# Index scores behind each query tile, a wider top-k search and six places for split weights in a hybrid decoder layer

## The chip, the cores and the metric

The kernel runs on one core of one Trainium2 chip, in one launch. The metric is the device time in microseconds; the kernel before took 826.19 us (median of three runs, 826.02 to 827.07).

## What is computed

One layer of an autoregressive trunk: 512 tokens of width 1024, float32, with a fixed memory of 256 tokens. The mixer has three head groups that read the same projection; this is its core, with the part that the change touches written out:

```python
h = layer_norm(x)
gq, gk, gv, glr, gg, dq, dk, dv, iq, ik, iw, sq, sk, sv = split(h @ w_in)
# indexer, per block of 128 query tokens
rel = relu(einsum('bthd,bsd->bths', iq, ik))          # 8 indexer heads of 64
isc = einsum('bths,bth->bts', rel, iw) * idx_scale
isc = where(causal, isc, -inf)
_, idx = top_k(isc, 128)                              # min(256, 512 // 4)
# sparse attention on the selected keys, less slope * distance
o_dsa = softmax(q @ k_sel - slopes * dist) @ v_sel @ w_uv
o_gla = gated_linear_attention(gq, gk, gv, glr, gg)   # 4 heads, chunks of 64
o_sb  = stick_breaking(sq, sk, sv)                    # 5 heads, strictly causal
h = layer_norm(ALPHA * h + concat(o_gla, o_dsa, o_sb) @ w_out)
h = layer_norm(ALPHA * h + mem_attention(h, mem))
h = layer_norm(ALPHA * h + relu(h @ w_up + b_up) ** 2 @ w_down + b_down)
```

Block 0 of the indexer needs no search: it has 128 keys, and all causal ones are taken.

## The kernel before

**Precision.** Weights and activations are split in a high and a low part. A product of two such operands is three matmuls on TensorE (PE): high x high, high x low, low x high (`mm3`). A weight chunk is loaded as a raw tile (`r_...`), copied to its high part (`h_...`, by ScalarE (ACT), GpSimd (POOL) or VectorE (DVE)), and the low part (`l_...`) is raw minus high (DVE or POOL). Raw tiles live in pool `wr` (4 places), high and low parts in `wh` and `wl` (5 places each, L383 and L384), temporaries of 512 floats in `half` (8 places), pages of 1024 floats in `pages` (31), and PSUM banks in `psum` (8). `page`, `temp` and `bank` take a tile from these.

**Order.** The code doesn't issue instructions as it runs. Every call on an engine is recorded by `Program` with the clock value of its place in the text; `nc.clock` can be set back or ahead, so that a piece of work is spread between others. `issue` then plans all instructions: it goes through time, picks for each engine the recorded operation that can start first by a table of prices and lags, at most 560 clock units ahead of the oldest that is not yet placed, holds a tile back until its pool has a place, and for operations recorded with `either` picks the engine. The instructions are emitted in that order from a single line, L356, which therefore stands in every row of the trace; each engine runs its queue in order and waits on semaphores. DMAs are issued from SyncE (SP).

**Stages.** The input layer norm, with its transposes, fills the first 25 us. Then come, by the order in the text: the indexer key and weights (`ik`, `iw`), the indexer queries (`iq`, four tiles of two heads each), the GLA values and gate rank (`gv_glr`), the GLA query-key tiles (`gqk_tile`, three of them), the score pages, the gates, GLA, stick-breaking (`sq`, `sk`, `ps_z`, `sp`), sparse attention (`ps_s`, `ps_pt`), output projection, memory attention (`ps_ms`, `ps_mpt`) and the MLP (`ps_up`, `ps_dn`).

**The indexer.** For each of the blocks j = 1, 2, 3 the page `acc` of that block, 128(j+1) columns wide, gathers eight heads: a pair of matmuls into a bank `ps_idx`, a relu on ACT into `r`, a multiply-add on DVE. All eight heads of all blocks are recorded behind the first query-key tile. `top_k` then finds 128 of the entries in 16 pairs of steps on DVE (MAX gives eight maxima, MATCH_REPLACE strikes them out), 17 clock steps a block, spaced by `TOPK_STRETCH` = 10 units; the mask that results copies key distances (`rel`) into the page `E`, which the sparse attention reads.

**GLA keys.** `gqk_tile` copies its bank to `gqk` and sends rows of it by DMA into `gqT` and `gkT`. `keT` is an exponential of the gate times `gkT`; `ps_ke` is its transpose on PE. `r_gg` and `r_sv` are weights of the gates and of the stick-breaking values, loaded on the same SP queue.

The lines of the changed parts:

Of the kernel before, what the change touches and what calls it, by code (L numbers as in the profile page):

```python
# [364 lines left out]
def trunk_kernel(ctx: ExitStack, tc: tile.TileContext, x, mem, ln_in_g, ln_in_b, w_in, gate_w2,  # L365
# [35 lines left out]
    def bank(name, shape=(512,)):  # L401
        return psum.tile([128] + list(shape), F32, name)
# [8 lines left out]
    def mm(o, a, b, start, stop):  # L411
        nc.tensor.matmul(o, a, b, start=start, stop=stop, skip_group_check=True)
# [27 lines left out]
                            base=0, channel_multiplier=1)  # L440


    scan_mask = cst.tile([128, 512], F32, "scan_mask")
    nc.gpsimd.memset(scan_mask, 1.0)
    nc.gpsimd.memset(scan_mask[:, 0:512:64], 0.0)
    ps = bank("ps_warm")
# [19 lines left out]
    def split_weights(raw, hi, lo):  # L466
        split(hi, lo, raw, slack[0])
# [95 lines left out]
    for t in range(NT):  # L563
        ln_hat(x_pg[t], "in")
        if t % 2:
            ln_transposed(x_pg, *gb_cols["in"], hT, t - 1, 2)


    rel = cst.tile([128, 512], F32, "rel")
    nc.gpsimd.iota(rel, pattern=[[1, 512]], base=-384, channel_multiplier=-1, allow_small_or_imprecise_dtypes=True)  # L570
    cmask_f = cst.tile([128, 128], F32, "cmask_f")
    nc.gpsimd.memset(cmask_f, 1.0)
    nc.gpsimd.affine_select(out=cmask_f, in_=cmask_f, pattern=[[1, 128]], compare_op=OP.is_ge, fill=0.0,
                            base=0, channel_multiplier=-1)
    nc.gpsimd.memset(cmask_f[0:64, 64:128], 0.0)
    cmask = cst.tile([128, 128], U32, "cmask")
    nc.vector.tensor_copy(cmask, cmask_f)
    tri_f = cst.tile([128, 128], F32, "tri_f")
    nc.gpsimd.memset(tri_f, -1.0)
    nc.gpsimd.affine_select(out=tri_f, in_=tri_f, pattern=[[-1, 128]], compare_op=OP.is_ge, fill=0.0,  # L580
                            base=0, channel_multiplier=1)
    negtri = cst.tile([128, 128], F32R, "negtri")
    nc.vector.tensor_copy(negtri, tri_f)
    ones_f = cst.tile([128, 128], F32, "ones_f")
    nc.gpsimd.memset(ones_f, -1.0)
    negones = cst.tile([128, 128], F32R, "negones")
    nc.vector.tensor_copy(negones, ones_f)
# [82 lines left out]
    gqT = page([2, T], F32, "gqT")  # L670
    gkT = page([2, T], F32, "gkT")
    for t in (gqT, gkT):
        nc.gpsimd.memset(t, 0.0)
    def gqk_tile(i):
        ps = proj_T([(C_GQ + 128 * i, 128, 0)], "gqk")
        raw = temp("gqk")
        for r0, r1 in (((0, 64), (64, 128)) if i == 1 else ((0, 128),)):
            is_q = 128 * i + r0 < C_GK
            nc.scalar.activation(raw[r0:r1], ps[r0:r1], AF.Copy, scale=GLA_DK ** -0.5 if is_q else 1.0)

        for n in range(2 * GLA_H):
# [9 lines left out]
    E_pg = [page([1024], F32, "E012"), page([512], F32, "E3")]
    E = [E_pg[0][:, 0:128], E_pg[0][:, 128:384], E_pg[0][:, 384:768], E_pg[1][:, 0:512]]
    accs = {}
    for j in range(1, NT):
        n = 128 * (j + 1)
        acc = temp(f"acc{j}")
        accs[j] = acc
        for h in range(IDX_H):
            ps = bank("ps_idx")
            for i in range(2):  # L700
                mm(ps[:, :n], iq[h][:, 128 * j:128 * j + 128], ik[:, i, 0:n], i == 0, i == 1)
            r = temp("r")
            nc.scalar.activation(r[:, :n], ps[:, :n], AF.Relu)
            if h == 0:
                nc.vector.tensor_scalar(acc[:, :n], r[:, :n], iw[:, j, 0:1], None, op0=OP.mult)
            else:
                nc.vector.scalar_tensor_tensor(acc[:, :n], r[:, :n], iw[:, j, h:h + 1], acc[:, :n],
                                               op0=OP.mult, op1=OP.add)
        nc.gpsimd.affine_select(out=acc[:, n - 128:n], in_=acc[:, n - 128:n], pattern=[[-1, 128]],
                                compare_op=OP.is_ge, fill=MASKED, base=0, channel_multiplier=1)  # L710

    def top_k(j):

        n = 128 * (j + 1)
        acc = accs[j]
        for _ in range(TOPK // 8):
            m8 = tiny(8, "m8")
            nc.vector.max(m8, acc[:, :n])
            nc.vector.match_replace(out=acc[:, :n], in_to_replace=m8, in_values=acc[:, :n], imm_value=TAKEN)
            yield  # L720
        msk = temp("msk", dtype=U32)
        nc.vector.tensor_scalar(msk[:, :n], acc[:, :n], -2e38, None, op0=OP.is_lt)
        nc.gpsimd.memset(E[j], MASKED)
        nc.vector.copy_predicated(E[j], msk[:, :n], rel[:, 384 - 128 * j:512])
        yield
# [22 lines left out]
    for p in range(2):  # L748
# [502 lines left out]
    def first_weights(i):  # L1251
        r0, r1 = raw_down(i, 0), raw_down(i, 1)
        t3 = temp("t3")
        any_tt(t3, r1[:, R], r0[:, R], OP.subtract)
        any_tt(r0[:, R], r0[:, R], r0[:, L], OP.subtract)
        kept = dram.tile([128, 1024], F32, f"t13_{i}")
        nc.sync.dma_start(kept[:, L], r0[:, R])
        nc.sync.dma_start(kept[:, R], t3)
        sums.append(kept)
        any_tt(r1[:, R], r1[:, R], r0[:, R], OP.subtract)  # L1260
        any_tt(r1[:, L], r1[:, R], r1[:, L], OP.subtract)
        hi = [wh_pool.tile([128, n], F32R, f"h_dn{n}") for n in (512, 1024)]
        lo = [wl_pool.tile([128, n], F32R, f"l_dn{n}") for n in (512, 1024)]
        split_weights(r0[:, L], hi[0], lo[0])
        split_weights(r1, hi[1], lo[1])
        return [(hi[0], lo[0]), (hi[1][:, R], lo[1][:, R]), (hi[1][:, L], lo[1][:, L])]
# [150 lines left out]
```

## Time and profile before

| | |
|---|---|
| median of three runs | 826.19 us (826.02 to 827.07) |
| profiled execution, device time | 825.4 us |
| its span in the trace | 823.6 us |
| granted TensorE clock, mean | 0.991 of full speed |
| PE busy | 792.5 us, 96% |
| DVE busy | 631.3 us, 77% |
| ACT busy | 329.2 us, 40% |
| POOL busy | 158.2 us, 19% |

The span is from the first to the last instruction of the profiled execution; the device time is 1.8 us longer. Busy PE is not PE at its peak: a stall of a matmul in its pipeline counts as busy. The waits of an engine tell what its idle time ended with. A clock of 1.00 is the full 2.4 GHz.

### The profile page before, as it was taken

To read this page: it belongs to the slowest core of one execution; us is meant where nothing else is said; L and a number is where in the kernel's file an instruction comes from. 1 tells how busy PE (TensorE), PEld (TensorE's weight loads), DVE (VectorE), ACT (ScalarE), POOL (GpSimd) and SP (SyncE) were. 2 spreads that over 40 slices of the span, in tenths; PEclk is the share of its full clock that TensorE was granted. 3 is DMA by queue.
4 is the path that set the end of the run, shared out by engine and by line. 5 is a ranking of instruction groups with operands and counts; after the bars stand their busy time and mean duration, and the time that the engine had idled before them with its cause. 6 is when DMAs were issued, how large, how long until landed. Compare 5 with 4: busy or idle time off the path is not lost.

```text
span 823.6 us, 11289 instructions
## 1 busy us (share of the span) xinstructions
PE 792.5 (96%) x4177; PEld 662.8 (80%) x4177; DVE 631.3 (77%) x1111; ACT 329.2 (40%) x634; POOL 158.2 (19%) x173
## 2 busy tenths in 40 slices
PE   7999999999999899989999989999999999899995
PEld 5997769777877888888878889888888888678884
DVE  7737999997649983886553799767777776798778
ACT  4506634577535540233330143333323232585420
POOL 5320142354622210227340210000000000110001
PEclk9999999999999999999999999999999999999998
DMA  8520331603244534023322024645546555467532
GB/s 239 137 53 15 100 94 27 179 9 103 75 152 159 165 120 150 27 77 103 114 92 77 26 77 142 217 154 186 197 137 214 196 174 175 138 219 240 196 126 103
DMA packets 99927, 106.70 MB, mean 130 GB/s; under 512 B 10448, under 2 KB 79136, under 8 KB 99872
## 3 DMA queue, kind: packets, MB, share of 16 engines
q1 hardware_dynamic: 97344, 99.00, 38.1%
q10 hardware_dynamic: 2528, 6.98, 2.5%
q8 instruction: 33, 0.54, 0.3%
q14 instruction: 22, 0.18, 0.1%
HBM read 94.69 MB, written 10.49 MB: 128 GB/s over the span
## 4 chain that ended last, share of the span: by engine, by line
PE 68%; DVE 16%; issue 2%; ACT 1%; DMA 1%; POOL 0%; DVEq 0%; ACTq 0%; POOLq 0%
PE ps_up L356 20%; PE ps_dn L356 17%; PE ps_wmo L356 4%; PE ps_wo L356 4%; PE ps_q L356 3%; DVE res L356 2%; PE ps_km L356 2%; PE ps_z L356 2%; DVE acc L356 2%; PE ps_vm L356 2%; PE ps_gg L356 1%; PE ps_dq L356 1%; PE ps_mo L356 1%; DVE m L356 1%; DVE s L356 1%
## 5 line engine op out<-in xcount | busy, mean ns | idle before, releaser
L356 PE MATMUL ps_up<-h2T,h_up 128*128 128x512 f32 (+1 forms) x576 | 161.1, 366 | 0.0
L356 PEld LDWEIGHTS ps_up<-h2T,h_up 128*128 128x128 f32 x576 | 104.0, 189 | 17.6 <-DVE h2T L356 0.2
L356 PE MATMUL ps_up<-h2T,l_up 128*128 128x512 f32 (+1 forms) x288 | 104.8, 366 | 0.5 <-DVE l_up L356 0.5
L356 ACT ACTIVATE ur<-ps_up,gb_all 128x512 f32<-128x512 f32 x32 | 22.1, 690 | 108.7 <-PE ps_up L356 108.7
L356 PEld LDWEIGHTS ps_up<-h2T,l_up 128*128 128x128 f32 x288 | 54.1, 189 | 9.5 <-DVE l_up L356 0.7
L356 PE MATMUL ps_dn<-h_dn,a 128*128 128x512 f32 x192 | 59.3, 389 | 0.0
L356 DVE TENSOR_TENSOR l_dn<-r_dn,h_dn 128x1024 fp32r<-128x1024 f32 (+1 forms) x44 | 45.2, 1026 | 5.1 <-ACT h_dn L356 3.7
L356 PE MATMUL ps_dn<-h_dn,ends 128*128 128x512 f32 x128 | 47.7, 396 | 0.7 <-DVE ends L356 0.7
L356 POOL TENSOR_TENSOR a<-keep,a 128x1024 fp32r<-128x1024 f32 x1 | 4.1, 4067 | 228.3 <-PE ps_dn L356 228.3
L356 PE MATMUL ps_q<-h1T,h_wmq 128*128 128x256 f32 (+1 forms) x192 | 45.7, 329 | 0.0
L356 ACT ACTIVATE h<-ps_lt,gb_all 128x256 f32<-128x256 f32 x20 | 10.2, 566 | 85.6 <-PE ps_lt L356 84.8
L356 PEld LDWEIGHTS ps_dn<-h_dn,a 128*128 128x128 f32 x192 | 36.0, 188 | 7.5
L356 PE MATMUL ps_wmo<-h_wmo,oT 128*128 128x512 f32 x128 | 40.7, 393 | 0.0
L356 DVE TENSOR_TENSOR l_up<-r_up,h_up 128x1024 fp32r<-128x1024 f32 x32 | 38.9, 1220 | 2.2 <-ACT h_up L356 0.5
L356 PE MATMUL ps_wo<-h_wo,mix 128*128 128x512 f32 x128 | 40.3, 392 | 0.0
L356 PE MATMUL ps_dn<-l_dn,a 128*128 128x512 f32 x96 | 37.3, 389 | 0.0
L356 PEld LDWEIGHTS ps_q<-h1T,h_wmq 128*128 128x128 f32 x192 | 32.9, 197 | 2.5 <-DVE h1T L356 0.2
L356 PE MATMUL ps_q<-h1T,l_wmq 128*128 128x256 f32 (+1 forms) x96 | 31.3, 330 | 0.5 <-DVE ve_mix L356 0.5
L356 DVE TENSOR_SCALAR h_up<-r_up 128x1024 fp32r<-128x1024 f32 x17 | 11.8, 692 | 26.1 <-PE ps_up L356 22.6
L356 PEld LDWEIGHTS ps_dn<-h_dn,ends 128*128 128x128 f32 x128 | 24.5, 192 | 6.3 <-DVE ends L356 1.2
L356 PEld LDWEIGHTS ps_wo<-h_wo,mix 128*128 128x128 f32 x128 | 24.0, 188 | 4.9
L356 PEld LDWEIGHTS ps_wmo<-h_wmo,oT 128*128 128x128 f32 x128 | 24.0, 188 | 4.8
(408 smaller groups left out, 2095.6 us busy)
## 6 DMA issues: line engine op xcount, KB each, us to landing
r_dn<-in_w_down_dram SPq DMA_DIRECT2D x48, 512.0 KB, 4.3
r_up<-in_w_up_dram SPq DMA_DIRECT2D x32, 512.0 KB, 4.5
r_t<-t SPq DMA_DIRECT2D x16, 512.0 KB, 3.6
r_kvv<-in_w_mem_kv_dram SPq DMA_DIRECT2D x8, 512.0 KB, 4.0
r_kvk<-in_w_mem_kv_dram SPq DMA_DIRECT2D x8, 512.0 KB, 3.6
r_wo<-in_w_out_dram SPq DMA_DIRECT2D x8, 512.0 KB, 4.4
r_wmq<-in_w_mem_q_dram SPq DMA_DIRECT2D x8, 512.0 KB, 5.0
r_wmo<-in_w_mem_o_dram SPq DMA_DIRECT2D x8, 512.0 KB, 3.4
```

What stands on the lines that cost most here:

```text
L356: f(*[real(a) for a in args], **{k: real(a) for k, a in kwargs.items()})
```

## The change

- `wh` and `wl` have six places each instead of five.
- Five constants give up their own room: `scan_mask` and `rel` share one page (`masks`), and `cmask_f`, `cmask`, `tri_f`, `ones_f` and `w2p` are temporaries.
- The transposes of the indexer weights `iw` come ahead of the queries. Each query tile (two heads) is followed by the scores of the two heads before it, for all three blocks; the scores of the last two heads come in `top_k`, ahead of the search of their block.
- Only the first two query tiles (h < 4) are computed in two halves of 256 columns; before it was three (h < 6).
- The search is recorded ahead of the GLA values, and its steps are spaced by 18 units instead of 10.
- All three GLA query-key tiles come behind the gate's exponentials; before, the first came ahead of the scores.
- In the MLP's down weights, the names and the order of four tile requests change.

The planner gives another order from this. The diff, cut to its core:

```diff
-    wh_pool = pool("wh", "wh", 5)
-    wl_pool = pool("wl", "wl", 5)
+    wh_pool = pool("wh", "wh", 6)
+    wl_pool = pool("wl", "wl", 6)
...
-    scan_mask = cst.tile([128, 512], F32, "scan_mask")
+    masks = page([2, 512], F32, "masks")
+    scan_mask, rel = masks[:, 0, :], masks[:, 1, :]
...
-    tri_f = cst.tile([128, 128], F32, "tri_f")
+    tri_f = temp("tri_f", 128)
...
     iq = new_q("iq", IDX_H)
-    for h in range(0, IDX_H, 2):
-        ps = proj_T([(C_IQ + 64 * h, 128, 0)], "iq", split=h < 6, weights=second if h == 0 else None)
-        for e in range(2):
-            stack(iq[h + e], ps, 64 * e, 1.0)
+    accs = {j: temp(f"acc{j}") for j in range(1, NT)}
+
+    def index_scores(h, j):
+        n, acc = 128 * (j + 1), accs[j]
+        ps = bank("ps_idx")
+        for i in range(2):
+            mm(ps[:, :n], iq[h][:, 128 * j:128 * j + 128], ik[:, i, 0:n], i == 0, i == 1)
+        r = temp("r")
+        nc.scalar.activation(r[:, :n], ps[:, :n], AF.Relu)
+        if h == 0:
+            nc.vector.tensor_scalar(acc[:, :n], r[:, :n], iw[:, j, 0:1], None, op0=OP.mult)
+        else:
+            nc.vector.scalar_tensor_tensor(acc[:, :n], r[:, :n], iw[:, j, h:h + 1], acc[:, :n],
+                                           op0=OP.mult, op1=OP.add)
+
+    def iq_tile(h):
+        ps = proj_T([(C_IQ + 64 * h, 128, 0)], "iq", split=h < 4, weights=second if h == 0 else None)
+        for e in range(2):
+            stack(iq[h + e], ps, 64 * e, 1.0)
+
+    for h in range(0, IDX_H, 2):
+        iq_tile(h)
+        if h:
+            for j in range(1, NT):
+                for e in range(2):
+                    index_scores(h - 2 + e, j)
...
+    def top_k(j):
+        n = 128 * (j + 1)
+        acc = accs[j]
+        for e in range(2):
+            index_scores(IDX_H - 2 + e, j)
...
-    start, nc.pace = nc.clock, GQK_PACE
-    gqk_tile(0)
-    nc.clock, nc.pace = start, 1.0
...
-    for i in range(1, 3):
+    for i in range(3):
         gqk_tile(i)
...
-TOPK_STRETCH = 10.0
+TOPK_STRETCH = 18.0
```

Three places of the order. A row is an instruction in the queue of its engine: output <- inputs, the shape, and xN for N alike in a row; numbers behind a name keep tiles of one name apart.

DVE where the search of the first page begins (block j = 1, 256 columns wide: `acc_773` before, `acc_558` after; `acc_867`, 384 wide, is that of block 2 before, `acc_576`, 512 wide, that of block 3 after). Before:

```order
64 L356 TENSOR_SCALAR h_gg<-r_gg 128x1024
65 L356 TENSOR_TENSOR l_gg<-r_gg,h_gg 128x1024
66 L356 SCALAR_TENSOR_TENSOR acc_773<-r,iw,acc_773 128x256 x7
67 L356 TENSOR_SCALAR acc_867<-r,iw 128x384
68 L356 SCALAR_TENSOR_TENSOR acc_867<-r,iw,acc_867 128x384
69 L356 MAX m_890<-acc_773 128x8
70 L356 SCALAR_TENSOR_TENSOR acc_867<-r,iw,acc_867 128x384
71 L356 MATCH_REPLACE acc_773<-m_890,acc_773 128x256
72 L356 SCALAR_TENSOR_TENSOR acc_867<-r,iw,acc_867 128x384
73 L356 MAX m_911<-acc_773 128x8
74 L356 SCALAR_TENSOR_TENSOR acc_867<-r,iw,acc_867 128x384
75 L356 MATCH_REPLACE acc_773<-m_911,acc_773 128x256
```

After:

```order
75 L356 SCALAR_TENSOR_TENSOR acc_566<-r,iw,acc_566 128x384
76 L356 SCALAR_TENSOR_TENSOR acc_576<-r,iw,acc_576 128x512
77 L356 SCALAR_TENSOR_TENSOR acc_558<-r,iw,acc_558 128x256
78 L356 SCALAR_TENSOR_TENSOR acc_576<-r,iw,acc_576 128x512
79 L356 TENSOR_TENSOR l_gqk<-r_gqk,h_gqk 128x1024
80 L356 SCALAR_TENSOR_TENSOR acc_558<-r,iw,acc_558 128x256
81 L356 MAX m_766<-acc_558 128x8
82 L356 MATCH_REPLACE acc_558<-m_766,acc_558 128x256
83 L356 MAX m_775<-acc_558 128x8
84 L356 MATCH_REPLACE acc_558<-m_775,acc_558 128x256
```

Before, the search alternated with the updates of the next page; now it starts after the last update of its own page and its pairs stand one behind the other.

SP's queue around the rows of the GLA keys (`gkT`), and DVE's queue ahead of `keT`. SP before:

```order
29 L356 DMA gqT<-gqk 48x512
30 L356 DMA gkT<-gqk 48x512
31 L356 DMA gkT<-gqk 16x512
32 L356 DMA gkT<-gqk 32x512
33 L356 DMA gkT<-gqk 48x512 x2
34 L356 DMA r_gg<-in_w_in_dram 128x8x128
35 L356 DMA r_sv<-in_w_in_dram 128x2x320 x4
```

SP after:

```order
29 L356 DMA gqT<-gqk 48x512
30 L356 DMA gkT<-gqk 48x512
31 L356 DMA gkT<-gqk 16x512
32 L356 DMA r_gg<-in_w_in_dram 128x8x128 x2
33 L356 DMA r_sv<-in_w_in_dram 128x2x320
34 L356 DMA gkT<-gqk 32x512
35 L356 DMA gkT<-gqk 48x512 x2
36 L356 DMA r_sv<-in_w_in_dram 128x2x320 x3
```

DVE after:

```order
122 L356 TENSOR_TENSOR keT<-bc 128x512
123 L356 TENSOR_TENSOR gqT<-gqT,grow 128x512 x2
124 L356 TENSOR_SCALAR h_gg<-r_gg 128x1024
125 L356 TENSOR_TENSOR l_gg<-r_gg,h_gg 128x1024
126 L356 TENSOR_SCALAR h_sv<-r_sv 128x640
127 L356 TENSOR_TENSOR keT<-gkT,keT 128x512
128 L356 TENSOR_TENSOR ktT<-gkT,ktT 128x512
129 L356 TENSOR_TENSOR keT<-gkT,keT 128x512
```

Before, all five `gkT` transfers stood ahead of the weights `r_gg` and `r_sv`; now two `r_gg` and one `r_sv` stand ahead of the last three, and on DVE the splits of `r_gg` and the high copy of `r_sv` stand ahead of the first product with `gkT`.

DVE ahead of the first stick-breaking scores, whose inputs are `sk` and `sq` from the bank `ps_skq` (`acc_954` before and `acc_576` after is the page of block 3, 512 wide). Before:

```order
213 L356 COPY_PREDICATED E_506<-msk,rel 128x384
214 L356 MATCH_REPLACE acc_954<-m_1656,acc_954 128x512
215 L356 TENSOR_TENSOR l_sk<-r_sk,h_sk 128x1024
216 L356 MAX m_1684<-acc_954 128x8
217 L356 TENSOR_TENSOR l_sq<-r_sq,h_sq 128x1024
218 L356 MATCH_REPLACE acc_954<-m_1684,acc_954 128x512
219 L356 TENSOR_TENSOR l_sk<-r_sk,h_sk 128x1024
220 L356 MAX m_1713<-acc_954 128x8
221 L356 TENSOR_TENSOR sk_1701<-ps_skq,sk_1701 64x512
222 L356 MATCH_REPLACE acc_954<-m_1713,acc_954 128x512
223 L356 SCALAR_TENSOR_TENSOR sq_1708<-ps_skq,sq_1708 64x512
224 L356 MAX m_1732<-acc_954 128x8
```

After:

```order
197 L356 TENSOR_TENSOR l_skq<-r_skq,h_skq 128x1024
198 L356 TENSOR_TENSOR l_sk<-r_sk,h_sk 128x1024
199 L356 TENSOR_TENSOR l_sq<-r_sq,h_sq 128x1024
200 L356 TENSOR_TENSOR l_sk<-r_sk,h_sk 128x1024
201 L356 TENSOR_SCALAR h_sq<-r_sq 128x1024
202 L356 TENSOR_TENSOR l_sq<-r_sq,h_sq 128x1024
203 L356 TENSOR_TENSOR sk_1641<-ps_skq,sk_1641 64x512
204 L356 SCALAR_TENSOR_TENSOR sq_1647<-ps_skq,sq_1647 64x512
205 L356 SCALAR_TENSOR_TENSOR acc_576<-r,iw,acc_576 128x512 x2
206 L356 MAX m_1693<-acc_576 128x8
207 L356 MATCH_REPLACE acc_576<-m_1693,acc_576 128x512
```

Nine pairs of the search of block 3 stood ahead of `sq` before, the last of them here between the splits; now the splits stand in one block and the search of block 3 begins behind `sq`.

## Rows read from the trace of the kernel before

**Rows 1.** The page's first part: busy us, share of the span, instructions

```profile
PE 792.5 (96%) x4177; PEld 662.8 (80%) x4177; DVE 631.3 (77%) x1111; ACT 329.2 (40%) x634; POOL 158.2 (19%) x173
```

**Rows 2.** Windows: stretch, length, busy us PE, PEld, DVE, ACT, POOL, clock

```profile
...
40.00:60.00 20.00, 20.00 (x108) 18.88 (x107) 8.13 (x10) 2.00 (x5) 5.97 (x5) 1.00 0.27 72
...
80.00:180.00 100.00, 96.53 (x514) 75.19 (x513) 98.15 (x233) 51.73 (x130) 30.24 (x32) 1.00 0.31 84
...
340.00:360.00 20.00, 17.59 (x103) 15.57 (x103) 19.70 (x32) 6.84 (x13) 6.88 (x7) 0.94 0.10 29
```

**Rows 3.** Waits of PE: waited for, us in total, times, longest us

```profile
...
PE ps_mpt L356 <- DVE mp L356: 1.7, 2, 1.2
PE ps_pt L356 <- DVE s L356: 1.6, 2, 1.0
PE ps_pt L356 <- DVE dst L356: 1.4, 2, 1.2
PE ps_z L356 <- DVE sp L356: 1.3, 2, 1.0
PE ps_ke L356 <- DVE keT L356: 1.1, 1, 1.1
PE ps_z L356 <- DVE sq L356: 0.8, 1, 0.8
```

**Rows 4.** Timeline of PE, query tiles: start us, duration us, instruction

```profile
34.08 0.28 PE L356 MATMUL ps_iq<-h0T,l_iq 128*128 128x256 f32 x1
34.44 0.28 PE L356 MATMUL ps_iq<-h0T,l_iq 128*128 128x256 f32 x1
...
39.71 0.39 PE L356 MATMUL ps_iq<-h0T,l_iq 128*128 128x512 f32 x1
...
40.40 0.39 PE L356 MATMUL ps_iq<-h0T,l_iq 128*128 128x512 f32 x1
```

**Rows 5.** Instructions on the score pages: duration ns min/median/max, first and last start

```profile
L356 DVE MAX8 m<-acc x48: 399/552/696, 72.8 to 173.3; 128x8 f32<-128x256 f32 x16, 128x8 f32<-128x384 f32 x16, 128x8 f32<-128x512 f32 x16
...
L356 DVE MATCH_REPLACE8 acc<-m,acc x48: 403/542/677, 73.7 to 174.7; 128x256 f32<-128x256 f32 x16, 128x384 f32<-128x384 f32 x16, 128x512 f32<-128x512 f32 x16
L356 DVE SCALAR_TENSOR_TENSOR acc<-r,iw,acc x21: 479/607/744, 65.8 to 85.8; 128x256 f32<-128x256 f32 x7, 128x384 f32<-128x384 f32 x7, 128x512 f32<-128x512 f32 x7
```

**Rows 6.** Timeline, splits of the stick-breaking weights on DVE and POOL

```profile
147.44 1.21 DVE L356 TENSOR_TENSOR l_sk<-r_sk,h_sk 128x1024 fp32r<-128x1024 f32 x1
...
150.03 2.61 POOL L356 TENSOR_TENSOR l_sq<-r_sq,h_sq 128x1024 fp32r<-128x1024 f32 x1 [5.18 <-ACT h_sq L356]
...
150.96 2.76 DVE L356 TENSOR_TENSOR l_sk<-r_sk,h_sk 128x1024 fp32r<-128x1024 f32 x1
```

**Rows 7.** Instructions on tile dst, which first read the masked distances

```profile
L356 DVE DVE_READ_ACCUMULATOR2_ANT dst<- x20: 77/82/84, 230.4 to 292.1; 128x1 f32 x20
```

**Rows 8.** Timeline around ps_ke; brackets give idle time before and its releaser

```profile
93.46 1.79 SPq L356 DMA_DIRECT2D gkT<-gqk  x3
...
95.98 7.31 SPq L356 DMA_DIRECT2D r_sv<-in_w_in_dram  x4
...
97.91 0.66 PE L356 MATMUL ps_ke<-ident,keT 128*128 128x128 f32 x4 [1.07 <-DVE keT L356]
```

**Rows 9.** Instructions on tile gkT: the issues, first and last start

```profile
L356 SPq DMA_DIRECT2D gkT<-gqk x5: 520/590/597, 87.5 to 94.7; - x5
```

**Rows 10.** DMA issues from 85 to 106 us: count, KB each, us to landing

```profile
r_sv<-in_w_in_dram SPq DMA_DIRECT2D x4, 320.0 KB, 4.8
...
gkT<-gqk SPq DMA_DIRECT2D x3, 96.0 KB, 2.2
```

**Rows 11.** Timeline of PE behind an idle time of 1.92 us

```profile
355.71 0.63 PE L356 MATMUL ps_lt<-ident,res 128*128 128x128 f32 x4 [1.92 <-DVE mv_mix L356]
...
359.09 0.63 PE L356 MATMUL ps_q<-h1T,h_wmq 128*128 128x256 f32 x2
...
359.73 0.63 PE L356 MATMUL ps_q<-h1T,h_wmq 128*128 128x256 f32 x2
```

More of the change, by code (lines that the diff above doesn't have):

```diff
@@ L566, in trunk_kernel @@
             ln_transposed(x_pg, *gb_cols["in"], hT, t - 1, 2)
-    rel = cst.tile([128, 512], F32, "rel")
     nc.gpsimd.iota(rel, pattern=[[1, 512]], base=-384, channel_multiplier=-1, allow_small_or_imprecise_dtypes=True)
[L571 to L577, printed above, removed]
-    tri_f = cst.tile([128, 128], F32, "tri_f")
+    tri_f = temp("tri_f", 128)
     nc.gpsimd.memset(tri_f, -1.0)
@@ L583, in trunk_kernel @@
     nc.vector.tensor_copy(negtri, tri_f)
-    ones_f = cst.tile([128, 128], F32, "ones_f")
+    ones_f = temp("ones_f", 128)
     nc.gpsimd.memset(ones_f, -1.0)
@@ L648, in trunk_kernel @@
     nc.scalar.activation(iwT[0:8, :], ps[64:72], AF.Copy, scale=IDX_SCALE)
-    iq = new_q("iq", IDX_H)
-    for h in range(0, IDX_H, 2):
-        ps = proj_T([(C_IQ + 64 * h, 128, 0)], "iq", split=h < 6, weights=second if h == 0 else None)
-        for e in range(2):
-            stack(iq[h + e], ps, 64 * e, 1.0)
     iw = cst.tile([128, NT, IDX_H], F32, "iw")
@@ L658, in trunk_kernel @@
     nc.scalar.copy(iw, ps)
+    iq = new_q("iq", IDX_H)
+    accs = {j: temp(f"acc{j}") for j in range(1, NT)}
[21 more added lines that the diff above has]
+                    index_scores(h - 2 + e, j)
+    E_pg = [page([1024], F32, "E012"), page([512], F32, "E3")]
+    E = [E_pg[0][:, 0:128], E_pg[0][:, 128:384], E_pg[0][:, 384:768], E_pg[1][:, 0:512]]
+    def top_k(j):
[3 more added lines that the diff above has]
+            index_scores(IDX_H - 2 + e, j)
+        nc.gpsimd.affine_select(out=acc[:, n - 128:n], in_=acc[:, n - 128:n], pattern=[[-1, 128]],
+                                compare_op=OP.is_ge, fill=MASKED, base=0, channel_multiplier=1)
+        for _ in range(TOPK // 8):
+            m8 = tiny(8, "m8")
+            nc.vector.max(m8, acc[:, :n])
+            nc.vector.match_replace(out=acc[:, :n], in_to_replace=m8, in_values=acc[:, :n], imm_value=TAKEN)
+            yield
+        msk = temp("msk", dtype=U32)
+        nc.vector.tensor_scalar(msk[:, :n], acc[:, :n], -2e38, None, op0=OP.is_lt)
+        nc.gpsimd.memset(E[j], MASKED)
+        nc.vector.copy_predicated(E[j], msk[:, :n], rel[:, 384 - 128 * j:512])
+        yield
+    start = nc.clock
+    for n, _ in enumerate(s for j in range(1, NT) for s in top_k(j)):
+        nc.clock = start + (n + 1) * TOPK_STRETCH
+    nc.clock = start
     gv = [page([2, 384], F32, f"gv{i}") for i in range(2)]
@@ L686, in gqk_tile @@
                 nc.sync.dma_start((gqT if n < GLA_H else gkT)[r:r + c1 - c0, p, :], raw[c0 - 128 * i:c1 - 128 * i])
-    start, nc.pace = nc.clock, GQK_PACE
-    gqk_tile(0)
-    nc.clock, nc.pace = start, 1.0
[L691 to L725, printed above, removed]
-    start = nc.clock
-    for n, _ in enumerate(s for j in range(1, NT) for s in top_k(j)):
-        nc.clock = start + (n + 1) * TOPK_STRETCH
-    nc.clock = start
-    w2p = cst.tile([16, 2, 2, 64], F32, "w2p")
+    w2p = temp("w2p", 256)[0:16].reshape(2, 2, 64)
     nc.gpsimd.memset(w2p, 0.0)
@@ L742, in trunk_kernel @@
     gb_cols["mix"], gb_cols["mem"] = gb_all[:2], gb_all[2:]
+    cmask_f = temp("cmask_f", 128)
+    nc.gpsimd.memset(cmask_f, 1.0)
+    nc.gpsimd.affine_select(out=cmask_f, in_=cmask_f, pattern=[[1, 128]], compare_op=OP.is_ge, fill=0.0,
+                            base=0, channel_multiplier=-1)
+    nc.gpsimd.memset(cmask_f[0:64, 64:128], 0.0)
+    cmask = temp("cmask", 128, U32)
+    nc.vector.tensor_copy(cmask, cmask_f)
     grow, ktT, keT = (page([2, T], F32, n) for n in ("grow", "ktT", "keT"))
@@ L1261, in first_weights @@
         any_tt(r1[:, L], r1[:, R], r1[:, L], OP.subtract)
[L1262 to L1266, printed above, removed]
+        left = [wh_pool.tile([128, 512], F32R, "h_dnl"), wl_pool.tile([128, 512], F32R, "l_dnl")]
+        hi, lo = wh_pool.tile([128, 1024], F32R, "h_dn"), wl_pool.tile([128, 1024], F32R, "l_dn")
+        split_weights(r0[:, L], *left)
+        split_weights(r1, hi, lo)
+        return [left, (hi[:, R], lo[:, R]), (hi[:, L], lo[:, L])]
     banks = {}
```

## The prediction, made before the changed kernel ran

> **What bounds the kernel now.** I read the busy times first: TensorE (PE) is busy 792.5 us, 96% of the span, so the reader looks for what takes PE's own work or its idle time, nothing else [rows 1]. Then the stretches: from 40 to 60 us VectorE (DVE) is busy 8.13 of 20 us, from 80 to 180 us 98.15 of 100, while PE is still busy 96.53 [rows 2]. So DVE is full in one stage, and before it more than half empty. Third, the waits of PE on DVE: the six that lie in the stages where the order changes sum to 1.7 + 1.6 + 1.4 + 1.3 + 1.1 + 0.8 = 7.9 us [rows 3]. That, and not DVE's busy time, is about all that moving DVE work can give back.
>
> **The sum is made against the profiled execution, 825.4 us** (span 823.6); the median of the runs shown is 826.19, 0.8 above it. What a measurement can tell from no change is 0.2%, 1.65 us: below 824.5 is faster, above 827.8 slower.
>
> **Part 1: the fourth query tile in one piece.** h = 4 is no longer cut in two halves of 256 columns. Three 256-column products pass in 34.44 - 34.08 = 0.36 us, three 512-column products in 40.40 - 39.71 = 0.69 [rows 4]. Per weight chunk 2 x 0.36 becomes 0.69, and there are eight chunks: 8 x 0.03 = 0.2. Taken: -0.2, bounds -0.3 and -0.1, since the starts are rounded to 0.01. The tile is copied out 512 columns wide either way.
>
> **Part 2: the index scores follow the query tiles.** 18 of the 24 updates of the score pages (0.48, 0.61 and 0.74 us by width [rows 5]) now stand between query tiles, in the stretch where DVE has 11.9 us of 20 free [rows 2]. 18 x 0.6 = 11 us fit into that. The search of the first page (16 pairs of MAX and MATCH_REPLACE, 0.40 + 0.40 and a load of 0.08 each [rows 5], so 14 us) starts when that page's last update is done, and stands in one block on DVE, where before it alternated with the updates of the next page. The price: PE's score products now stand between weight products, and wait for ScalarE to empty a bank or for a query tile to be stacked. In the trace the same kind of product stands where all its inputs are old, so no row shows this wait. Below, it is nothing (a product that comes just in time). Above, I take each of three later query tiles' stacks as costing one wait of the size of the ones seen, 0.8 [rows 3], thus 2.4. I take +0.3: PE has the products of the next tile queued ahead in the order, and the scores follow two heads late, so the value lies near the lower end.
>
> **Part 3: the search is spread wider.** The stretch from 10 to 18 puts the third page's 16 pairs later: in the order, nine of them stood ahead of the first stacked query of the stick-breaking stage (sq), now none; instead three more steps of weight splitting stand there, two of them at 1.21 us [rows 6] and a copy that is cheaper. 9 x (0.69 + 0.68 + 0.08) = 13.0, less 2.4 and the copy, makes DVE's queue ahead of sq some 10 us shorter. The wait for sq (0.8) then goes: -0.8. It had a second cause that goes too: one of the splits of sk took 2.76 us while GpSimd (POOL) ran a split of 2.61 beside it, against 1.21 alone [rows 6], and POOL's split of sq now stands on DVE. Bounds -0.8 and 0.
>
> The nine pairs come back after sq, among the first stick-breaking heads: the third page is finished some 13 us of DVE work later. Its page is first read at about 230 us [rows 7], so its own lateness costs nothing, but the sa and sp steps of the first head now share DVE with it. The order has the first sp step 10 us of DVE work earlier, and the next ones about where they were. So of the 1.3 us that PE waits for sp [rows 3] I take half away: -0.6, bounds -1.3 and +1.0 (one more wait of the size seen, rounded).
>
> **Part 4: softmax and memory attention, ps_pt and ps_mpt.** The waits of 1.6, 1.4 and 1.7 us [rows 3] end with DVE's scaling of a softmax row. Ahead of these steps the order has 0.1 to 2.8 us less DVE work, but DVE was idle between, so most of the lead is lost. I take -0.8 of 3.0 and -0.4 of 1.7, a quarter each; bounds all of it (-4.7) and +1.0.
>
> **Part 5: the GLA keys, ps_ke.** PE waits here 1.07 us for keT [rows 8]. The chain behind it: three DMAs of gkT from 93.46, then keT, then ps_ke at 97.91, 4.45 us after their issue began [rows 8]. Two things move. PE gets there earlier: three products of the gate (0.69 [rows 4]), four score products of 512 columns (0.9) and one of 384 (0.2) now stand behind it, and the 0.2 of part 1 is gone, 2.0 us in all: it arrives at 97.91 - 1.07 - 2.0 = 94.8. And SyncE's queue is new: two r_gg, one r_sv of 512, 512 and 320 KB now stand ahead of the last three gkT, where before r_gg and r_sv came behind them; on DVE the splits of that r_gg and of r_sv stand ahead of keT and wait for those weights to land. The last query-key tile is projected earlier too, by about 3 us of PE work, so that by the 4.45 us alone keT would be ready as PE arrives. But DVE first needs the weights: r_sv, issued behind r_gg from 95.98 on, takes 4.8 us to land [rows 8, 10]. In the new order it goes out behind the middle tile's gkT copies, the first of which goes out at 87.5 in the trace [rows 9], so near 89. Landing, the copy of r_sv and keT (some 0.7 us each, as the widest update of [rows 5]) then end at 95.2, and up to 96.8 if the two r_gg ahead hold the landing longer: a wait between 0.4 and 2.0, of which I take 1.4, nearer the upper end for the second r_gg. That is +0.3 against now, bounds -1.1 (no wait) and +2.4 (below).
>
> The gkT DMAs, 96 KB each, land 2.2 us after issue when no weights stand ahead of them, and r_sv, with 512 KB of r_gg ahead, takes 4.8 [rows 10]. The Trainium skill (DMA: Bandwidth & Descriptors, Queues, rings and completion order) has SyncE's DMAs on one ring of each of 16 engines, consumed in ring order, so gkT would stand behind all 1344 KB rather than pass them. By that rule, at the pace of r_sv's landing (512 + 320 KB in 4.8 - 2.2 = 2.6 us), the weights and the last gkT need 4.5 + 2.2 = 6.7 us from about 89, keT ends at 96.4 and the wait is 1.6, so a term of +0.5 in place of +0.3; were it false, DVE's queue alone would set the wait.
>
> **Part 6: six places for split weights.** From the MLP on, the order on PE and DVE is the same row for row, and so is the stall before the end. Cost 0; bounds -1 and +1 for shifts in landing. The room comes from constants: masks in a shared page, the others copied to a temporary once. The same steps with the same shapes: 0.
>
> **Sum:** -0.2 + 0.3 - 0.8 - 0.6 - 0.8 - 0.4 + 0.3 = -2.2, profiled 823.2. With 0.8 for the median: **824.0 us**, this case's own range 821.5 to 825.4.
>
> **Rivals.**
> *Slower: keT behind the weights.* If r_gg and r_sv hold DVE and gkT more than I take, PE idles at ps_ke about 2.1 us, +1.0. After an idle of 1.92 us the granted clock of the stretch 340 to 360 us was 0.94 (1.2 GHz in part of it), and three 256-column products took 0.64 rather than 0.36 us [rows 2, 4, 11]; over some five such triples that is +1.4. The stretch with the wait of 1.07 us kept 1.00 [rows 2, 8]. So the mechanism decides at keT 1.9 us behind PE, that is 96.7 us. With +0.5 for new score waits and only part 1 gained: +1.0 + 1.4 + 0.5 - 0.2 = +2.7, 828.1, median 828.9. For it: the two weights ahead, on both queues. Against: the query-key tile is 3 us earlier.
>
> *No gain: the waits are chains, not backlog.* The waits for s, dst and mp end in steps that follow PE's own result by ScalarE and DVE; a shorter queue does not shorten them. Then only -0.2 and -0.8 hold, and the score waits (+0.5) and ps_ke (+0.3) eat them: -0.2, 825.2, median 826.0. For it: DVE is not full after 180 us. Against: the stage up to 180 us, where it is.
>
> *All DVE waits go.* 7.9 us of waits and 0.2: 817.3, median 818.1. For it: DVE's queue is lighter in all six places. Against: DVE's steps after 180 us are unmoved.
>
> **How the numbers follow.** The forecast has 0.50 (0.34 of it below 824.5, 0.16 within 0.2%), no gain 0.17, all waits gone 0.14, slower 0.19. Faster is 0.34 + 0.14 = 0.48, same 0.16 + 0.17 = 0.33, slower 0.19. The range goes down to 820.0, leaving out most of the case in which all waits go, and up to 828.5, leaving out the upper half of the slower one.
>
> **What would show it.** Part 1: three products in 0.69 us throughout the fourth tile. Part 2: no PE wait over 0.8 us between 36 and 60 us, and the first MAX near 57 us instead of 72.8 [rows 5]. Part 3: no wait for sq and no 2.76 us split. Part 5: the wait at ps_ke and the clock behind it. Part 6: the MLP's waits as before. A wait of PE over 1.9 us before 230 us, or new waits among the query tiles of over 2 us in all, would make the prediction wrong.

## The result, and the profile after

The changed kernel takes **833.42 us** (median of four runs, 832.82 to 833.74) against 826.39 for the kernel before beside it: a ratio of 1.0084 (95% interval 1.0068 to 1.0100), slower by some 7 us. The forecast was 824.0 with a range of 820.0 to 828.5. Its profiled execution took 833.18 us, with a span of 831.5 and a mean clock of 0.986.

The page's first lines answer to [rows 1]. PE has 798.4 us of busy time where it had 792.5, and its share is the same 96%: a reader who stops at the shares sees nothing.

```profile
span 831.5 us, 11235 instructions
...
PE 798.4 (96%) x4153; PEld 664.9 (80%) x4153; DVE 636.9 (77%) x1112; ACT 329.5 (40%) x634; POOL 154.3 (19%) x172
```

The waits of PE answer to [rows 3]: engine, what waited, for whom, us in total, times, longest. Those for sq, sp, s and dst are gone from the list. Those for mp and keT have grown, and one at ps_A is new.

```profile
PE ps_mpt L356 <- DVE mp L356: 6.4, 5, 2.0
...
PE ps_ke L356 <- DVE keT L356: 2.3, 1, 2.3
...
PE ps_A L356 <- issue: 1.1, 1, 1.1
```

Where the time went is read from the first start of three of PE's tiles, which stand in both traces: the projection of the stick-breaking queries (ps_skq), the scores of the memory attention (ps_ms) and the MLP (ps_up). Before, they began at 144.8, 370.2 and 475.8 us; after, at 152.1, 372.3 and 482.9. So 7.3 us are lost up to 144, 5.2 of them are won back by 370, and 5.0 are lost again in memory attention. Two losses with a gain between them look, in the total, like one loss. The rows of the three tiles (duration in ns, then first and last start), before and after:

```profile
L356 PE MATMUL ps_skq<-h0T,h_skq x16: 389/389/397, 144.8 to 149.8; 128*128 128x512 f32 x16
...
L356 PE MATMUL ps_ms<-kms,qT x96: 277/283/385, 370.2 to 426.6; 128*128 128x256 f32 x96
...
L356 PE MATMUL ps_up<-h2T,h_up x576: 278/389/397, 475.8 to 708.6; 128*128 128x512 f32 x149, 128*128 128x256 f32 x43
```

```profile
L356 PE MATMUL ps_skq<-h0T,h_skq x16: 389/389/398, 152.1 to 157.1; 128*128 128x512 f32 x16
...
L356 PE MATMUL ps_ms<-kms,qT x96: 278/283/283, 372.3 to 433.7; 128*128 128x256 f32 x96
...
L356 PE MATMUL ps_up<-h2T,h_up x576: 278/389/397, 482.9 to 715.2; 128*128 128x512 f32 x149, 128*128 128x256 f32 x43
```

These starts do not stand behind quite the same work. In the changed kernel four score products of 512 columns (0.9 us) come only after the first ps_skq, and eleven products of ps_q of 256 columns (1.3 us, at three in 0.36 [rows 4]) come ahead of the first ps_ms: 126 of the 288 ps_q stand there, and 115 before. For equal work, then, the first loss is some 8.2 us, the gain 7.4 and the second loss 6.3. Every kernel with six places has these eleven products ahead of ps_ms, and none with five.

**The first loss, at the GLA keys.** The timeline (start, duration, engine, instruction; in brackets the idle time before it and its releaser), which answers to [rows 8]:

```profile
87.25 1.17 SPq L356 DMA_DIRECT2D gkT<-gqk  x2
...
88.52 2.05 SPq L356 DMA_DIRECT2D r_gg<-in_w_in_dram  x2
...
90.66 1.18 SPq L356 DMA_DIRECT2D r_sv<-in_w_in_dram  x1
...
91.94 1.80 SPq L356 DMA_DIRECT2D gkT<-gqk  x3
...
95.99 0.49 DVE L356 TENSOR_SCALAR h_sv<-r_sv 128x640 fp32r<-128x640 f32 x1 [0.71 <-DMA r_sv<-in_w_in_dram]
...
96.40 0.68 DVE L356 TENSOR_TENSOR keT<-gkT,keT 128x512 f32<-128x512 f32 x1
...
96.62 1.88 POOL L356 TENSOR_TENSOR l_sv<-r_sv,h_sv 128x640 fp32r<-128x640 f32 x1 [31.77 <-DVE h_sv L356]
...
97.01 2.03 DVE L356 TENSOR_TENSOR ktT<-gkT,ktT 128x512 f32<-128x512 f32 x1
...
97.23 0.63 PE L356 MATMUL ps_ke<-ident,keT 128*128 128x128 f32 x4 [2.28 <-DVE keT L356]
...
99.14 0.76 PE L356 MATMUL ps_A<-gqT,ktT 48*128 48x128 f32 x2 [1.05 <-issue]
```

PE reaches ps_ke at 97.23 - 2.28 = 94.95, as forecast (94.8), but keT is not there: r_sv went out at 90.66, and not near 89, DVE waited for it until 95.99, and keT stood behind it. The transfers of gkT were late as well, which [rows 10] have at 2.2 us from issue to landing:

```profile
gkT<-gqk SPq DMA_DIRECT2D x3, 96.0 KB, 3.8
...
gkT<-gqk SPq DMA_DIRECT2D x1, 64.0 KB, 4.3
```

Then ktT took 2.03 us beside POOL's l_sv, against 0.68 in the trace before, and PE waited again for 1.05 us, until just after ktT's end at 99.04. Behind the two waits the clock fell. The windows (stretch, length, busy time of PE, PEld, DVE, ACT, POOL, then the clock) have it at 0.62 of full speed for 9 us, some of it at the lower level of 1.2 GHz; 9 x 0.38 = 3.4 us of PE's time at most:

```profile
90.00:97.00 7.00, 4.95 (x23) 3.87 (x21) 3.62 (x5) 1.80 (x3) 0.38 (x1) 1.00 0.98 288
97.00:106.00 9.00, 7.71 (x36) 6.11 (x36) 7.95 (x16) 3.17 (x8) 3.03 (x2) 0.62 0.55 134
106.00:135.00 29.00, 28.97 (x144) 18.55 (x143) 21.40 (x63) 10.53 (x53) 9.31 (x10) 1.00 0.20 54
```

The same stretches before kept the clock at 1.00:

```profile
97.00:106.00 9.00, 8.09 (x43) 5.44 (x43) 8.80 (x28) 4.34 (x9) 5.58 (x4) 1.00 0.67 203
106.00:135.00 29.00, 28.82 (x177) 21.80 (x177) 28.08 (x81) 11.15 (x53) 9.54 (x9) 1.00 0.30 73
```

The growth of the wait (1.2), the new wait (1.05) and the clock (3.4 at most; e5 puts it near 1.5) make 3.8 to 5.7 of the 7.3 us. The rest isn't assigned to a wait. It lies in the GLA stage behind them: from 106 to 135 us, at the full clock in both traces, PE is busy throughout and gets through 144 products where it had 177.

**The second loss, in memory attention.** The timeline of the third memory head:

```profile
414.42 4.70 POOL L356 TENSOR_TENSOR l_wmo<-r_wmo,h_wmo 128x1024 fp32r<-128x1024 f32 x2
...
414.94 4.85 DVE L356 TENSOR_SCALAR mp<-mp,mst 128x256 f32<-128x256 f32 x4
...
416.97 0.44 PE L356 MATMUL ps_mpt<-ident,mp 128*128 128x128 f32 x2 [1.97 <-DVE mp L356]
...
419.32 1.08 PE L356 MATMUL ps_mpt<-ident,mp 128*128 128x128 f32 x4 [1.91 <-DVE mp L356]
```

Four scalings of a softmax row take DVE 4.85 us. Among the sixteen of the trace, the row of the tile has a median of 354 ns and a longest of 2439:

```profile
L356 DVE TENSOR_SCALAR mp<-mp,mst x16: 333/354/2439, 378.4 to 435.8; 128x256 f32<-128x256 f32 x16
```

POOL's pair of subtractions l_wmo runs beside them. In POOL's order before the change each l_wmo followed its own h_wmo; with six places POOL makes two copies, and then two subtractions in a row. Before:

```profile
408.93 1.91 POOL L356 TENSOR_SCALAR h_wmo<-r_wmo 128x1024 fp32r<-128x1024 f32 x1
410.93 2.37 POOL L356 TENSOR_TENSOR l_wmo<-r_wmo,h_wmo 128x1024 fp32r<-128x1024 f32 x1
```

After, ahead of the pair shown above:

```profile
411.52 2.93 POOL L356 TENSOR_SCALAR h_wmo<-r_wmo 128x1024 fp32r<-128x1024 f32 x2
```

The third head accounts for 3.9 of the 6.4 us of waits for mp. The other 2.5 are the first head's, whose scalings of 1.14, 1.12 and 2.44 us stand beside POOL's two h_wmq and the first of its two l_wmq; before, none of that head's took over 0.41.

### The profile page after: what moved, and what is told of

Same layout as the page of the kernel before. It is cut to its first block, busy times and chain, and to the rows that moved or that the text cites. A ratio compares the mean times of both kernels' runs of the same rounds, so it can differ in the third digit from the quotient of the medians.

```text
span 831.5 us, 11235 instructions
## 1 busy us (share of the span) xinstructions
PE 798.4 (96%) x4153; PEld 664.9 (80%) x4153; DVE 636.9 (77%) x1112; ACT 329.5 (40%) x634; POOL 154.3 (19%) x172
## 4 chain that ended last, share of the span: by engine, by line
PE 83%; DVE 12%; ACT 2%; issue 2%; DMA 1%; POOL 1%; SPq 0%; DVEq 0%; ACTq 0%; POOLq 0%
PE ps_up L356 20%; PE ps_dn L356 17%; PE ps_wmo L356 4%; PE ps_wo L356 4%; PE ps_q L356 3%; PE ps_vm L356 3%; PE ps_iq L356 3%; PE ps_z L356 3%; PE ps_gv_glr L356 2%; PE ps_gg L356 2%; DVE res L356 2%; PE ps_km L356 2%; PE ps_sv L356 2%; PE ps_dq L356 1%; PE ps_sq L356 1%
## 5 line engine op out<-in xcount | busy, mean ns | idle before, releaser
L356 DVE TENSOR_TENSOR l_dn<-r_dn,h_dn 128x1024 fp32r<-128x1024 f32 x28 | 34.2, 1222 | 3.6 <-ACT h_dn L356 2.4
L356 DVE TENSOR_SCALAR h_dn<-r_dn 128x1024 fp32r<-128x1024 f32 x14 | 9.7, 694 | 34.0 <-PE ps_up L356 33.8
L356 DVE MAX8 m<-acc 128x8 f32<-128x256 f32 (+2 forms) x48 | 26.8, 559 | 2.1 <-POOL acc L356 0.9
L356 PE MATMUL ps_dn<-h_dn,mid 128*128 128x512 f32 x64 | 25.4, 397 | 1.9 <-ACT mid L356 1.9
```

The source lines that it names most:

```text
L356: f(*[real(a) for a in args], **{k: real(a) for k, a in kwargs.items()})
```

## The experiments

The edits of the order are made behind the planner, on its finished list: the instructions named are put later, with what depends on them, and all else keeps its place. Edits of a number let the planner order anew. The second column is the median with the ratio to the kernel before; the last three are how late each tile began against the trace of before, in the profiled execution. That is one execution: e2's took 2.7 us more than its kernel's median, e8's 1.9 less.

| kernel | us | ratio (95%) | ps_skq | ps_ms | ps_up |
|---|---|---|---|---|---|
| changed kernel | 833.42 | 1.0084 (1.0068 to 1.0100) | +7.3 | +2.1 | +7.1 |
| e1 gkT ahead of the weights | 846.61 | 1.0261 (1.0231 to 1.0290) | +19.9 | +14.7 | +22.8 |
| e2 l_wmo pair on DVE | 826.40 | 1.0010 (0.9998 to 1.0022) | +8.4 | +3.2 | +4.1 |
| e3 five places | 831.04 | 1.0066 (1.0051 to 1.0081) | +7.7 | +4.8 | +4.4 |
| e4 before, six places | 838.30 | 1.0147 (1.0127 to 1.0168) | +11.1 | +6.7 | +12.9 |
| e5 idle times filled | 831.96 | 1.0065 (1.0050 to 1.0080) | +5.9 | +0.8 | +6.7 |
| e6 filled, l_wmo on DVE | 825.59 | 0.9992 (0.9982 to 1.0002) | +4.6 | -0.5 | +0.2 |
| e7 stretch 10 | 843.92 | 1.0213 (1.0198 to 1.0229) | +17.2 | +11.9 | +18.3 |
| e8 tile 0 first | 830.16 | 1.0056 (1.0038 to 1.0074) | +1.8 | -1.6 | +3.4 |
| e9 tile 0 first, l_wmo on DVE | 823.33 | 0.9971 (0.9962 to 0.9980) | +1.3 | -2.4 | -1.5 |
| e10 the same, wmq off POOL | 823.46 | 0.9974 (0.9964 to 0.9985) | +1.7 | -1.9 | -0.8 |
| e11 tile 0 first, five places | 828.42 | 1.0036 (1.0015 to 1.0056) | +1.6 | +2.1 | +1.8 |

**e1, the wait at ps_ke taken away.**

```diff
  SP
-DMA r_gg<-in_w_in_dram x2
-DMA r_sv<-in_w_in_dram
 DMA gkT<-gqk x3
+DMA r_gg<-in_w_in_dram x2
+DMA r_sv<-in_w_in_dram
  DVE: h_gg, l_gg and h_sv likewise behind keT and ktT
```

> The changed kernel, with the planner's order edited at one place: the two r_gg and the one r_sv transfer go behind the last gkT transfer on SP, and DVE's h_gg, l_gg and h_sv behind keT and ktT. Everything else is the changed kernel's order. Theory (the weights ahead hold keT, and the idle time that follows lowers the clock): the waits at ps_ke (2.28 us) and at ps_A (1.05) go, and so does the low clock from 97 to 105 us (about 2 us): 833.4 - 5 = 828.4, clock 1.00 in 100 to 120 us. Rival (PE only waits elsewhere, since the gate's products need those weights soon): the gate's products wait instead, gain under 1.5 us, above 832.

The wait went (ps_ke began 1.5 us earlier), and the kernel became 13 us slower: the rival's bound of 832 was passed, but neither theory had this outcome. PE now waited 1.54 us for ket and 1.34 for an ACT step, and behind these the clock stayed low through 40 us of the interleaved GLA stage:

```profile
100.00:120.00 20.00, 18.44 (x55) 11.80 (x55) 12.78 (x32) 5.43 (x20) 8.26 (x7) 0.54 0.43 112
120.00:140.00 20.00, 20.00 (x57) 11.12 (x56) 7.64 (x24) 3.11 (x20) 1.53 (x2) 0.61 0.00 1
```

By these rows the clock weighs more here than the waits, which are 2.9 us in all; no run separates the two in this order. Why the clock came back after some 9 us in the changed kernel and after 40 here is open.

**e2, POOL's pair on DVE.**

```diff
  POOL
-TENSOR_TENSOR l_wmo<-r_wmo,h_wmo x2
  DVE
 TENSOR_TENSOR oT<-ps_mo,oT
+TENSOR_TENSOR l_wmo<-r_wmo,h_wmo x2
```

> The changed kernel, with two of POOL's l_wmo subtractions (the pair of 4.7 us from 414.4) moved to DVE behind the oT step of the next stage; nothing else is moved. Theory (DVE's four softmax scalings mp, 0.35 us each alone, took 4.85 us because POOL's subtraction ran beside them): mp takes 1.4 us, the two waits at ps_mpt (1.97 and 1.91) shrink to under 1 us together, and the clock stays 1.00 there: 833.4 - 4.5 = 829. Rival (the scalings are late because of the chain of scores, maxima and exponentials ahead of them): mp stays late by over 3 us, time within 1 us of 833.4.

The theory held for the waits, and the gain was larger than forecast. POOL's two copies h_wmo end at 416.73, nothing of POOL's stands beside the scalings, and the four take 1.12 us together; PE's wait for them is 0.39:

```profile
417.22 1.12 DVE L379 TENSOR_SCALAR mp<-mp,mst 128x256 f32<-128x256 f32 x4
...
417.61 0.96 PE L379 MATMUL ps_mpt<-ident,mp 128*128 128x128 f32 x6 [0.39 <-DVE mp L379]
```

The medians differ by 7.0 us. In the profiled execution the stage from ps_ms to ps_up is 4.1 us shorter (+0.9 behind against +5.0); the other 2.9 are not located there, since that execution (829.08) was itself 2.7 above this kernel's median.

**e3 and e4, the places alone.** e3 sets both pools back to five; e4 is the kernel before with six, and with the constants moved as the change moves them.

> The changed kernel with five places for split weights instead of six; the planner orders it anew. Its POOL queue has each l_wmo behind its own h_wmo, as before the change, and its SP queue has r_gg, r_gg and r_sv ahead of gkT, as the changed kernel. Theory (two losses, of which the six places cause the one in memory attention): that one, 5.0 us between 384 and 430 us, goes, the one of GLA stays: 828.5, +7 against before at 144 us and +2 to +3 at the end. Rival (the places have nothing to do with it): 833.

> The kernel before with six places and the constants' room from the change, and nothing else of it. Theory: POOL's pair of l_wmo stands beside the softmax scalings again, a loss of 4 to 5 us between 384 and 430 us, and one r_gg and one r_sv ahead of the last gkT only cost up to 1: 830 to 832. Rival (six places are free): 826.

Both theories held for memory attention: with five places ps_up is 0.4 us ahead of ps_ms's lateness, with six it is 6.2 behind. In e3 the first loss stays (+7.7), and its total of 831.04 lies between its two forecasts. In e4 the wait at ps_mpt has the changed kernel's size. Its total missed the forecast by 6, since the new order costs GLA another 11 us (a wait of 4.1 us at ps_sv for a weight's copy). What I had not expected stands in e3's list of waits: those for s and dst are back at their size of [rows 3].

```profile
PE ps_pt L356 <- DVE s L356: 1.6, 2, 1.0
PE ps_pt L356 <- DVE dst L356: 1.4, 2, 1.2
```

So the six places give 2.7 us by ps_ms (+2.1 against +4.8) and take 5.4 behind it (+5.0 against -0.4). e11 and e8, the same pair with tile 0 first, say 3.7 and 5.3. For equal work of PE (the eleven ps_q) it is 4.0 and 6.7, and 5.0 and 6.6. What is left in the medians is a cost of 2.4 us (e3) or 1.7 (e11).

**e5 and e6, PE kept busy through the idle times.**

```diff
 MATMUL ps_idx<-ik,iq 128x384
+MATMUL ps_idx<-ik,iq 128x384 x12
 MATMUL ps_ke<-ident,keT
...
+MATMUL ps_idx<-ik,iq 128x384 x5
 MATMUL ps_A<-gqT,ktT
```

> The changed kernel with more work for PE and nothing less: the last score product ahead of ps_ke (384 columns, which starts its bank anew, so repeating it gives the same bank) is repeated 12 times there and 5 times ahead of the first ps_A, 17 x 0.165 = 2.8 us in the two idle times of 2.28 and 1.05 us. Theory (the idle times cost twice, once as waits and once by the clock that falls behind them): the clock stays 1.00 from 97 to 106 us, where the trace of the changed kernel shows 0.76, 0.50 and 0.96, and the time falls by about 2 to 3 us though PE does more: 831. Rival (the clock falls for another reason, or costs nothing): 833 to 834.

> Both edits in one: the repeated score product in the two idle times at the GLA keys, and POOL's pair of l_wmo moved to DVE. Theory: the gains add up, 826.4 (the second alone) - 2.5 = 824, faster than the kernel before by 2. Rival (the second edit's gain of 7 us had the clock of the GLA stage in it already): 826 to 827.

The clock stayed at 1.00 in all three stretches, with 2.8 us more work on PE, and the time fell by 1.5 us in the medians:

```profile
97.00:106.00 9.00, 8.41 (x55) 6.47 (x53) 8.71 (x17) 4.17 (x14) 3.43 (x2) 1.00 0.57 149
```

That the idle times lower the clock, and that this costs time, is shown. The repeats (2.8 us) stand for about as much idle time: PE waits 0.6 us at ps_ke and ps_A where it waited 3.3. So the 1.5 us are about the price of the clock, under half of the 3.4 that the windows allowed. And they are not the whole loss: with those waits and the low clock gone, ps_skq still begins 5.9 us late, 3.1 after the repeats are taken off, and the GLA stage is as slow as in the changed kernel:

```profile
106.00:135.00 29.00, 28.98 (x145) 18.95 (x145) 22.90 (x66) 10.28 (x50) 9.32 (x10) 1.00 0.22 59
```

Why PE takes that long there without a wait and at the full clock is open. e6 came out between its theory and its rival: 825.59, level with the kernel before, with ps_skq still 4.6 us late.

**e7, the spread set back to 10.** One constant.

> The changed kernel with the search spread by 10 units, as before the change; the planner orders it anew. One r_gg instead of two and a r_sv stands ahead of the last gkT, and POOL still has its pair of l_wmo. Theory (the spread and the places are separate causes): the memory attention loses its 4 to 5 us as the changed kernel does, the GLA stage less, and waits for sq come back (0.8): 830 to 832. Rival (the spread has nothing to do with GLA): 833 to 835.

Both sides missed: 843.9. With the old spread in the new order PE waits 5.9 us at ps_ke, and the clock is 0.67 and 0.69 in the stretches 97 to 106 and 106 to 135. The wider spread isn't what made the change slow; without it this order is 10.5 us slower. The wait for sq, which the theory had back, did not return, although all sixteen pairs of block 3 stand ahead of sq in e7; PE is 17.2 us late there.

**e8, the first query-key tile ahead again.**

```diff
+    start, nc.pace = nc.clock, GQK_PACE
+    gqk_tile(0)
+    nc.clock, nc.pace = start, 1.0
...
-    for i in range(3):
+    for i in range(1, 3):
         gqk_tile(i)
```

> The changed kernel with the first GLA query-key tile recorded ahead of the rest again, as before the change; the planner orders it anew. SP still has a r_gg and a r_sv ahead of the last three gkT, one r_gg less than the changed kernel. Theory (what stands ahead of gkT and keT sets the wait): keT comes about 1 us earlier against PE, the wait at ps_ke is 1 to 1.5 and the clock stays: 830 to 831, with the loss in memory attention as it was. Rival: the wait stays over 2 us, 833.

The theory held: the wait at ps_ke is back at 1.0, the clock stays, and the first loss shrinks from 7.3 to 1.8 us, with r_gg and r_sv still ahead of gkT. That was its fastest execution of ten; the median is 3.3 us below the changed kernel's. The second loss is as it was. The planner orders anew here, so the place of tile 0 is shown to decide most of the first loss, but not which step of the new order does it.

```profile
PE ps_mpt L356 <- DVE mp L356: 6.3, 5, 1.9
...
PE ps_ke L356 <- DVE keT L356: 1.0, 1, 1.0
...
97.00:106.00 9.00, 8.54 (x62) 6.68 (x63) 8.04 (x21) 3.60 (x17) 3.73 (x3) 1.00 0.73 201
```

**e9, both repairs,** e8 with the edit of e2.

> The kernel with the first query-key tile ahead (830.2), and POOL's pair of l_wmo moved to DVE as before. Theory: the two repairs act in different stages and add up; the pair costs the 3.9 us of waits at ps_mpt and the clock behind them, 4 to 7 us: 823 to 826, faster than the kernel before or level with it. Rival (the 7 us of the earlier edit were mostly an undisturbed clock in the GLA stage, which this kernel has already): 827 to 829.

823.33 us: this version beats the changed kernel by 10 us and the kernel before by 0.29% (0.20 to 0.38). Its start of ps_ms is 2.4 us ahead of before, about the gain that the prediction had in mind, and memory attention gives back 0.9 of it instead of 5.0.

**e10 and e11.** e10 takes the first memory head's splits off POOL as well; e11 is e8 with five places.

> The same with POOL's two h_wmq and two l_wmq of the first memory head off POOL as well (copies to ACT, subtractions to DVE behind oT). In the trace of the kernel with the tile ahead, the softmax scalings of that head took 1.14, 1.12 and 2.43 us, each ending just after POOL's instruction, and PE waited 0.5, 0.5 and 1.5 us for them. Theory: these 2.4 us go too, 2 us less than the run without this edit, 821 to 824. Rival (PE needs those weights, so that it waits for them instead): no gain.

> The kernel with the first query-key tile ahead and five places instead of six; the planner orders it anew. Its POOL queue has each l_wmo behind its own h_wmo. Theory (the two causes are separate): the GLA stage as with six places, memory attention without the pair's collision: 826 to 828, 2 to 4 less than 830.2. Rival (the places matter elsewhere too): 830.

e10 missed: no gain. That is the rival's number for another reason, since PE waits for none of those weights. With its old work gone, POOL began the next weights (wmo) at once, and the scalings met these:

```profile
374.33 4.08 DVE L384 TENSOR_SCALAR mp<-mp,mst 128x256 f32<-128x256 f32 x4
374.38 1.19 POOL L384 TENSOR_SCALAR h_wmo<-r_wmo 128x1024 fp32r<-128x1024 f32 x1
...
375.65 2.35 POOL L384 TENSOR_TENSOR l_wmo<-r_wmo,h_wmo 128x1024 fp32r<-128x1024 f32 x1
```

e11 came out just above the theory's range (828.42). It has neither tile 0 late nor six places, and it is still slower than the kernel before, by 0.36% (0.15 to 0.56).

## Why the prediction was wrong

- **Part 6 failed.** It priced six places at 0, because the order from the MLP on is the same row for row. But places for weights act where weights are split, and memory attention splits eight wmq and eight wmo chunks. I did not look at POOL's order there. By the start of the MLP it cost 5.0 us, more than the whole sum, through DVE's softmax scalings standing beside POOL's splits (e2 and e3 show the cause). Net of what the six places give ahead of it, 2.4 us are left (e3).
- **Part 5 failed by more.** Its term was +0.3, and 7.3 us were lost there. PE's arrival was right to 0.2 us. The wait was taken as 1.4 and came out at 2.28, because r_sv went out 1.7 us later than I had it and took 5.3 us to DVE's start, not 4.8. That is past the 1.9 us at which the rival was to decide, and the clock fell as the rival had it; its price for that, 1.4, agrees with the 1.5 of e5. The term left out ktT, the next step on DVE, which met POOL's split and cost PE 1.05, and it left out the GLA stage behind, which is slower without a wait and at the full clock by some 3 us (e5). That last cause stays open. The rival had a total of 828.9 and a chance of 0.19; what neither it nor the sum had took the time past it.
- **The rule of the Trainium skill weighed in part 5** (DMA: Bandwidth & Descriptors, Queues, rings and completion order) gave a wait of 1.6, nearer than my 1.4. The trace agrees that gkT is held up behind the weights: three took 3.8 us to land instead of 2.2, the first 4.3, so from 91.94 to near 96.2. DVE, released by r_sv at 95.99, was done with h_sv some 0.4 us later, so both ways end at about the same time, and it isn't shown which alone would have set the wait.
- **Part 4 had the wrong sign for ps_mpt** (-0.4, measured +4.7 in the list of waits), for the reason of part 6. For ps_pt it had -0.8; both waits, 3.0, went. e3 and e11 have them back with five places, so the six places did this and not a lighter DVE queue: the right sign by luck.
- **Part 3 had its number, and its reason is not shown.** The waits for sq and sp are gone (0.3 us for POOL's sk stand in their place). But e7, at the old spread, has no wait for sq either. Between ps_skq and ps_ms 5.2 us are won back, against 2.2 in the sum for sq, sp and ps_pt; 2.7 of the 5.2 are the six places' (e3).
- **Parts 1 and 2 held.** The tile h = 4, the third of the four, runs its products at three in 0.69 us. The first MAX began at 57.4 us (57 was forecast), and no wait on a score product is in the list.
- **The gain was not there without the six places.** Parts 1 to 4 add up to -2.5, and e11 has neither the six places nor tile 0 late; yet it is 0.36% slower than before. Only e9 and its variant e10, with six places and both repairs, are faster.

What the sum lacked was a check of every stage in which a pool's tiles live, and a look at PE's pace in the GLA stage, where busy time hides what is lost.

## What to carry to other kernels

When a pool of tiles gets a place more, compare the order of every engine in every stage that uses the pool, not only the stage that the change names: the work that comes free early lands somewhere, here beside the softmax scalings. In this kernel, whose PE is 96% busy, waits of 2.28 and 1.05 us were paid again in clock, at some 1.5 us, and in e1's order the clock stayed low for 40; so count the clock in the price of a wait. Compare starts of tiles only after counting what work stands ahead of each. And a repair that only shifts the wait (e1, e10) can cost as much as the fault: look at what the freed engine does next.

## What the runs showed of the hardware

In these traces DVE's scaling of a 128x256 row (one SBUF input, a scalar from SBUF) does not share time with POOL's 1024-wide operations: 0.35 us alone, and beside them each of the long ones ends some 0.15 us after POOL's instruction. The first of the four above took 1.98 us, to 416.92, with POOL's first subtraction ending at 414.42 + 2.35 = 416.77:

```profile
414.94 1.98 DVE L356 TENSOR_SCALAR mp<-mp,mst 128x256 f32<-128x256 f32 x1
...
414.42 2.35 POOL L356 TENSOR_TENSOR l_wmo<-r_wmo,h_wmo 128x1024 fp32r<-128x1024 f32 x1
```

The next POOL instruction then got in before DVE's second scaling. The Trainium skill (SBUF — State Buffer, Who interferes with whom) says that the two engines share a pair of ports, that whichever starts first holds it for its whole instruction, and that `tensor_scalar` is among the operations that can want it; the trace agrees.
